# An edge of order on VectorE: each expert block's rest behind the fetched rows already issued

## The chip, the cores and the metric

The kernel runs on one core of a Trainium2 chip. The metric is the device time of one execution in microseconds, the median of several runs. Engines are named as the profile names them: PE (TensorE), DVE (VectorE), ACT (ScalarE), POOL (GpSimd), SP (SyncE).

## The reference

One decoder layer on 1024 tokens of width 1024, in float32, followed by a last RMSNorm. The first half mixes tokens; the second is a retrieval of single-neuron experts, and only that half matters here:

```
def peer(h, w_query, sub_keys1, sub_keys2, expert_down, expert_up):
    q = (hf @ w_query).reshape(T, 8, 2, 128)
    s1, s2 = scores of both halves against 128 keys each
    v1, i1 = top_k(s1, 16); v2, i2 = top_k(s2, 16)
    top_s, pos = top_k(all 256 sums v1 + v2, 16)
    idx = i1 * 128 + i2 at pos          # 16 of 16384 experts, for each of 8 heads
    gates = softmax(top_s)
    # for each token t, over its 8 * 16 = 128 chosen experts e:
    out[t] = sum_e gates[t, e] * gelu(h[t] . expert_down[e]) * expert_up[e]
```

Then x + gate_f * out, and the last norm.

## The kernel before

The 1024 tokens are eight tiles of 128. Two ways of computing the experts run side by side.

Dense tiles (1, 2, 3, 4; 512 tokens). The 16384 experts are 128 blocks of 128. For each block (loop over `units` in `experts`, 1 or 3 blocks to a unit) SP loads the block's down weights (`raw`, L1021) and up weights (`up`, L1029). ACT copies `raw` to float32r (`dnh`, L1023), and DVE takes the rest that this rounding left, `raw - dnh` (`dnl`, L1024): this instruction is what the text calls the rest. PE multiplies (L1033) `dnh` by the high part of h, `dnl` by the high part, `dnh` by the low part, 8 matmuls each, in this order. ACT applies Gelu (L1036), DVE multiplies by the gates (L1037), and one unit later `mm2` (L1007) multiplies by `up`. Half of its outputs stay in PSUM (`res`), the other half (`rot`) are added to SBUF sums by DVE (`ys`, L1014). There are three `raw` buffers and two each of `dnh` and `dnl`.

Fetched tiles (0, 5, 6, 7). For each of a token's 128 experts, one indirect DMA issued by POOL fetches a row of 8 KB (down and up) for each of 128 tokens, so 128 x 8 KB = 1.05 MB: this is what the text calls a row (`gather`, L907). DVE multiplies the down half by h and sums (the dot, L910), ACT applies Gelu and the gate (L911, L912), DVE adds the weighted up half to `yacc` (the add, L903; L901 for the first row of a tile). The add of a row is written in the program after the dot of the next. There are four row buffers (`ROWBUFS` + `MORE`); a row's buffer is free for the next fetch when its add is done. Tile 0 is fetched in `ahead` (half rows), most of it during the first half of the kernel; tiles 5, 6, 7 are fetched beside the dense blocks, 3 x 128 = 384 rows.

What sets the order. Each engine runs its instructions in one fixed order, which the scheduler writes from the priorities of the program. The rows are background work: `drain` takes steps of the generators in `self.bg` at a priority lower by 2000, after each dense block. After b blocks, `min(450 * b / 122, 450)` steps have been issued (L1043 to L1045; `steps` is 129 * 4 - 106 + 40, where 106 is the number of steps of `ahead` that the earlier stages have taken, and NK - SB * LEAD is 122). Those 450 steps are 23 left of `ahead`, 40 of the selections, and 129 for each of the three fetched tiles. Issued means written in the program; the low priority lets the scheduler place a row later than a block written behind it.

After the last block `mm2` runs for the last unit, and `finish` scales, adds and normalises the dense tiles.

Of the kernel before, what the change touches and what calls it, by code (L numbers as in the profile page):

```python
# [6 lines left out]
FT = mybir.dt.float32  # L7
# [6 lines left out]
OP = mybir.AluOpType  # L14
# [3 lines left out]
D = 1024  # L18
# [47 lines left out]
class Trunk:  # L66
    def __init__(self, ctx, tc, I, out):
        self.ctx, self.tc, self.nc, self.I, self.out = ctx, tc, tc.nc, I, out
        self.bg = []
        self.due, self.owed, self.few = 0, 0, 2  # L70
        self.early, self.taken = None, 0

    def pool(self, name, bufs=1, **kw):
        return self.ctx.enter_context(self.tc.tile_pool(name=name, bufs=bufs, **kw))
# [17 lines left out]
    def fetch(self, n):  # L92

        if not self.early or self.pending:
            return
        self.owed += n
        while self.owed >= 1:
            self.owed -= 1
            with self.tc.high_priority(offset=-LATER):
                if next(self.early, None) is None:  # L100
                    return
            self.taken += 1


    def consts(self):
# [782 lines left out]
    def gather(self, j):  # L888

        nc, gp = self.nc, self.gp  # L890
        t = GT[j]
        h2 = gp.tile([128, D], FT, name="h2", bufs=1)
        nc.sync.dma_start(h2, self.h2r[j * 128:(j + 1) * 128, :])
        acc = gp.tile([128, D], FT, name="yacc")
        e = self.eidx[:, j - EARLY].rearrange("p a b -> p (a b)")
        g = self.gates[:, j].rearrange("p a b -> p (a b)")
        prev = None

        def add(u, a, s):
            if s == 0:  # L900
                nc.vector.tensor_scalar(acc, u[:, D:], a, None, op0=OP.mult)  # L901
            else:
                nc.vector.scalar_tensor_tensor(acc, u[:, D:], a, acc, op0=OP.mult, op1=OP.add)  # L903

        for s in range(128):
            u = self.row()
            nc.gpsimd.indirect_dma_start(out=u, out_offset=None, in_=self.I["ud"],  # L907
                                         in_offset=bass.IndirectOffsetOnAxis(ap=e[:, s:s + 1], axis=0))
            a = gp.tile([128, 1], FT, name="act", bufs=4)
            nc.vector.scalar_tensor_tensor(u[:, :D], u[:, :D], 1.0, h2, op0=OP.mult, op1=OP.mult, accum_out=a)  # L910
            nc.scalar.activation(a, a, AF.Gelu)  # L911
            nc.scalar.activation(a, a, AF.Copy, scale=g[:, s:s + 1])  # L912
            if prev is not None:
                add(*prev)
            prev = (u, a, s)
            yield
        add(*prev)
        rows = self.last_rows()
        if j == len(GT) - 1:
            self.kept = rows  # L920
            self.rows.pop()
        xx = self.row()
        self.finish(t, [acc[:, :512], acc[:, 512:]], rows, self.residual(xx[:, :D], t), xx[:, D:])
        yield
# [29 lines left out]
    def experts(self):  # L954

        nc, I = self.nc, self.I
# [10 lines left out]
        def new(kind):  # L967
            return pools[kind].tile(*kinds[kind][:2], name=kind)
# [24 lines left out]
        def mm2(u, ws, some=outs):  # L993
            for o in some:
                t, h = o
                ps = held[o] if o in held else rot.tile([128, 512], FT, name="rot")
                hs = slice(h * 512, (h + 1) * 512)
                ts = slice(t * 128, (t + 1) * 128)
                n = 0
                whole = u == last and o in ysum  # L1000
                if whole:
                    nc.tensor.matmul(ps, self.ident, ysum[o], start=True, stop=False, skip_group_check=True)
                for w, up in ws:
                    st = n == 0 and (u == 0 or o in ysum) and not whole
                    n += 1
                    sp = n == len(ws) and (u == last or o in ysum)
                    nc.tensor.matmul(ps, w[:, ts], up[:, hs], start=st, stop=sp, skip_group_check=True)  # L1007
                if whole:
                    sums[o] = ps
                elif o in ysum:  # L1010
                    if u == 0:
                        nc.vector.tensor_copy(ysum[o], ps)
                    else:
                        nc.vector.tensor_tensor(ysum[o], ps, ysum[o], op=OP.add)  # L1014

        b = 0
        for u, size in enumerate(units):
            ws = []
            for j in range(size):
                raw = new("raw")  # L1020
                nc.sync.dma_start(raw, I["downT"][b])  # L1021
                dn = new("dnh"), new("dnl")
                nc.scalar.activation(dn[0], raw, AF.Copy)  # L1023
                nc.vector.tensor_tensor(dn[1], raw, dn[0].bitcast(FT), op=OP.subtract)  # L1024
                if b % GS == 0:
                    gates = new("gates")
                    nc.sync.dma_start(gates, self.gd[b // GS])
                up = new("up")
                nc.sync.dma_start(up, I["ud"][b * 128:(b + 1) * 128, D:])  # L1029
                p1 = pm1.tile([128, 512], FT, name="m1")  # L1030
                for n, (x, y) in enumerate(((0, 0), (1, 0), (0, 1))):
                    for k in range(KB):
                        nc.tensor.matmul(p1, dn[x][:, k * 128:(k + 1) * 128], h2[y][:, k],  # L1033
                                         start=(k == 0 and n == 0), stop=(k == KB - 1 and n == 2))
                act = new("w")
                nc.scalar.activation(act, p1, AF.Gelu)  # L1036
                nc.vector.tensor_tensor(act.rearrange("p (c t) -> p c t", t=TC),  # L1037
                                        act.rearrange("p (c t) -> p c t", t=TC), gates[:, :, b % GS], op=OP.mult)
                ws.append((act, up))
                if queue and j == (u == last):  # L1040
                    mm2(*queue.pop())
                b += 1
                want = min(steps * b // (NK - SB * LEAD), steps)  # L1043
                self.drain(want - done)
                done = want  # L1045
            queue.append((u, ws))
# [94 lines left out]
```

## Time and profile before

| | |
|---|---|
| time, median of 3 runs | 2900.75 us (2895.56 to 2902.41) |
| the profiled execution's own time | 2912.44 us |
| its span in the trace | 2910.6 us |
| PE busy | 2663.1 us, 91% |
| DVE busy | 2375.6 us, 82% |
| POOL busy | 884.6 us, 30% |
| ACT busy | 830.1 us, 29% |
| moved by DMA | 893.31 MB, mean 307 GB/s |

The profiled execution is one of its own, 11.7 us above the median of the runs; sums are made against its span. The trace gives each instruction's start, duration and line, and the idle time of an engine before it with what ended that idle time. The expert loop begins near 1221 us with the first rest and its last matmuls end near 2891 us.

### The profile page before, as it was taken

Reading aid. Unit: us, or ns where it says so; the run is one execution under the profiler, and the core shown is the slowest. Engines: PE = TensorE matmul, PEld = TensorE weight load, DVE = VectorE, ACT = ScalarE, POOL = GpSimd, SP = SyncE. Lnnn points to the kernel's source line nnn. Section 1 sums busy time; section 2 is a strip of 40 time slices with the busy share of each in tenths; the row PEclk is TensorE's granted clock in tenths of the full one; section 3 lists DMA queues with packets and bytes.
Section 4 is the critical chain, followed back from the end, with each engine's and each line's share of the span. In section 5 each row is a group of like instructions: output and inputs, shape, how many; then the busy total and the mean of one; then the engine's idle time right before and its main releaser. Section 6 shows DMA issues by size and latency. Waiting matters only on the chain. (4 is left out here: it accounts for less than half of the span.)

```text
span 2910.6 us, 31644 instructions
## 1 busy us (share of the span) xinstructions
PE 2663.1 (91%) x10243; PEld 1746.7 (60%) x10244; DVE 2375.6 (82%) x5156; ACT 830.1 (29%) x2244; POOL 884.6 (30%) x679
## 2 busy tenths in 40 slices
PE   8899986789889989699999999999999999999961
PEld 5688555676557876465655666666666666666630
DVE  6625898979999879899999777787877777778887
ACT  3523451322254342322222222222222222222211
POOL 0000066554440005022333333333333333333343
PEclk9999987899989989899999999999999999999985
DMA  8655389999863679888999999899999989998986
GB/s 304 222 172 173 103 296 331 356 362 361 289 234 124 185 220 383 277 310 323 352 354 356 356 366 337 336 364 361 346 348 351 370 320 372 348 368 339 356 320 234
DMA packets 264278, 893.31 MB, mean 307 GB/s; under 512 B 25904, under 2 KB 110000, under 8 KB 212656
## 3 DMA queue, kind: packets, MB, share of 16 engines
q0 software_dynamic: 92448, 541.11, 49.0%
q1 hardware_dynamic: 171664, 350.18, 34.7%
q8 instruction: 81, 1.33, 0.2%
q14 instruction: 85, 0.70, 0.1%
HBM read 840.86 MB, written 50.34 MB: 306 GB/s over the span
## 5 line engine op out<-in xcount | busy, mean ns | idle before, releaser
L907 POOL DMA_INDIRECT row<-in_ud,eidx x384 | 547.5, 1426 | 1105.8 <-DVE yacc L903 870.4
L903 DVE SCALAR_TENSOR_TENSOR yacc<-row,act,yacc 128x1024 f32<-128x1024 f32 x381 | 488.5, 1282 | 67.9 <-ACT act L912 65.1
L910 DVE SCALAR_TENSOR_TENSOR row<-row,h 128x1024 f32<-128x1024 f32 x384 | 467.1, 1218 | 51.1 <-DMA row<-in_ud,eidx 50.8
L1007 PE MATMUL rot<-up,w 128*128 128x512 f32 x1024 | 464.5, 596 | 4.8 <-DVE ys L1014 4.8
L1007 PE MATMUL res<-up,w 128*128 128x512 f32 x1024 | 458.6, 592 | 0.0
L870 POOL DMA_INDIRECT row<-in_ud,eidx x256 | 313.6, 1225 | 417.3 <-DVE rkb L777 102.1
L911 ACT ACTIVATE act<-act 128x1 f32<-128x1 f32 x384 | 77.1, 201 | 976.0 <-DVE row L910 975.6
L1007 PEld LDWEIGHTS rot<-up,w 128*128 128x128 f32 x1024 | 194.9, 191 | 221.8 <-issue 208.3
L1007 PEld LDWEIGHTS res<-up,w 128*128 128x128 f32 x1024 | 193.8, 189 | 200.5 <-issue 189.4
L1033 PE MATMUL m<-h2h,dnh 128*128 128x512 f32 x1024 | 292.9, 427 | 18.9 <-ACT dnh L1023 18.9
L1033 PE MATMUL m<-h2l,dnh 128*128 128x512 f32 x1024 | 285.6, 413 | 0.0
L1033 PE MATMUL m<-h2h,dnl 128*128 128x512 f32 x1024 | 279.6, 412 | 0.0
L1033 PEld LDWEIGHTS m<-h2h,dnh 128*128 128x128 f32 x1024 | 193.5, 189 | 96.8 <-issue 39.5
L307 PE MATMUL acc<-wraw,r 128*128 128x256 f32 x1024 | 239.3, 388 | 8.3 <-ACT s L525 8.3
L435 PE MATMUL acc<-r,wraw 128*128 128x384 f32 (+1 forms) x768 | 235.0, 464 | 2.3 <-ACT s L439 1.3
L581 PE MATMUL acc<-rz,wraw 128*128 128x384 f32 (+1 forms) x768 | 235.3, 457 | 0.0
L1033 PEld LDWEIGHTS m<-h2l,dnh 128*128 128x128 f32 x1024 | 192.6, 188 | 66.5 <-issue 30.4
L1033 PEld LDWEIGHTS m<-h2h,dnl 128*128 128x128 f32 x1024 | 193.4, 189 | 59.2 <-issue 19.1
L307 PEld LDWEIGHTS acc<-wraw,r 128*128 128x128 f32 x1024 | 196.3, 195 | 37.9 <-ACT s L525 9.9
L1014 DVE TENSOR_TENSOR ys<-rot,ys 128x512 f32<-128x512 f32 x168 | 115.4, 687 | 112.1 <-PE rot L1007 111.6
L435 PEld LDWEIGHTS acc<-r,wraw 128*128 128x128 f32 x768 | 147.7, 195 | 81.8 <-issue 8.6
L581 PEld LDWEIGHTS acc<-rz,wraw 128*128 128x128 f32 x768 | 143.7, 194 | 64.0 <-issue 2.3
(298 smaller groups left out, 3271.3 us busy)
## 6 DMA issues: line engine op xcount, KB each, us to landing
up<-in_ud SPq DMA_DIRECT2D x128, 512.0 KB, 7.4
raw<-in_downT SPq DMA_DIRECT2D x128, 512.0 KB, 7.9
gd<-stage SPq DMA_DIRECT2D x32, 1024.0 KB, 9.3
gates<-gd SPq DMA_DIRECT2D x16, 2048.0 KB, 12.3
wraw<-in_w_c SPq DMA_DIRECT2D x48, 512.0 KB, 5.6
wraw<-in_w_q SPq DMA_DIRECT2D x48, 512.0 KB, 6.3
wraw<-in_w_o SPq DMA_DIRECT2D x36, 512.0 KB, 5.2
row<-in_w_ada SPq DMA_DIRECT2D x32, 512.0 KB, 5.3
```

Of the source, the lines that this page charges most:

```text
L307: self.nc.tensor.matmul(acc[i], a(4 * kp + j, slice(i * 128, (i + 1) * 128)), ws[:, j * 256:(j + 1) * 256], start=kp == kps[0] and j == 0 ...
L435: nc.tensor.matmul(acc[:, :T], wc[:, k * 128:(k + 1) * 128], h[:, k], start=k == 0, stop=k == KB - 1)
L581: nc.tensor.matmul(acc[:, :T], wq[:, k * 128:(k + 1) * 128], g[:, k], start=k == 0, stop=k == KB - 1)
L870: nc.gpsimd.indirect_dma_start(out=u[:, i * D:(i + 1) * D], out_offset=None, in_=src, in_offset=bass.IndirectOffsetOnAxis(ap=e[:, s + i:s ...
L903: nc.vector.scalar_tensor_tensor(acc, u[:, D:], a, acc, op0=OP.mult, op1=OP.add)
L907: nc.gpsimd.indirect_dma_start(out=u, out_offset=None, in_=self.I["ud"], in_offset=bass.IndirectOffsetOnAxis(ap=e[:, s:s + 1], axis=0))
L910: nc.vector.scalar_tensor_tensor(u[:, :D], u[:, :D], 1.0, h2, op0=OP.mult, op1=OP.mult, accum_out=a)
L911: nc.scalar.activation(a, a, AF.Gelu)
L1007: nc.tensor.matmul(ps, w[:, ts], up[:, hs], start=st, stop=sp, skip_group_check=True)
L1014: nc.vector.tensor_tensor(ysum[o], ps, ysum[o], op=OP.add)
L1033: nc.tensor.matmul(p1, dn[x][:, k * 128:(k + 1) * 128], h2[y][:, k], start=(k == 0 and n == 0), stop=(k == KB - 1 and n == 2))
```

## The change

An instruction edge of the kind that only sets order (no semaphore, both ends on the same engine) is drawn from each block's rest to the last add of a fetched row that the program has issued before it. `mark` is that last add, L901 or L903; it is None until the first row of tile 5 has been added, so the first blocks get no edge. Rows of tile 0, fetched in `ahead`, don't set it. No instruction is added or taken away.

```diff
+        self.mark = None
...
+    def after(self, ins, prev):
+
+        self.tc.add_manual_dep(ins.ins, prev.ins.name,
+                               mybir.DependencyInfo(mybir.DependencyClass.NoSync, mybir.DependencyReason.DATA),
+                               reason="order")
...
             if s == 0:
-                nc.vector.tensor_scalar(acc, u[:, D:], a, None, op0=OP.mult)
+                self.mark = nc.vector.tensor_scalar(acc, u[:, D:], a, None, op0=OP.mult)
             else:
-                nc.vector.scalar_tensor_tensor(acc, u[:, D:], a, acc, op0=OP.mult, op1=OP.add)
+                self.mark = nc.vector.scalar_tensor_tensor(acc, u[:, D:], a, acc, op0=OP.mult, op1=OP.add)
...
-                nc.vector.tensor_tensor(dn[1], raw, dn[0].bitcast(FT), op=OP.subtract)
+                rest = nc.vector.tensor_tensor(dn[1], raw, dn[0].bitcast(FT), op=OP.subtract)
+
+                if self.mark is not None:
+                    self.after(rest, self.mark)
```

## Rows read from the trace of the kernel before

**Rows 1.** Busy time of all engines by stretch of the expert loop. Columns: stretch and its length in us, busy us and number of instructions of each engine, granted TensorE clock, share of DMA time, GB/s.

```profile
1221.00:1642.00 421.00, 415.87 (x1348) 256.44 (x1349) 392.44 (x934) 102.75 (x255) 126.03 (x92) 0.99 0.91 346
1642.00:1966.80 324.80, 324.80 (x1050) 197.60 (x1048) 251.00 (x323) 76.29 (x206) 111.20 (x77) 1.00 0.91 348
1966.80:2709.40 742.60, 742.60 (x2406) 453.26 (x2405) 578.02 (x729) 175.19 (x471) 245.71 (x174) 1.00 0.92 352
2709.40:2777.40 68.00, 68.00 (x218) 40.85 (x217) 54.92 (x70) 15.59 (x44) 26.15 (x18) 1.00 0.92 350
2777.40:2811.00 33.60, 33.14 (x96) 17.78 (x95) 28.81 (x38) 6.08 (x23) 15.55 (x10) 1.00 0.87 315
2811.00:2881.50 70.50, 0.00 (x0) 0.00 (x0) 54.05 (x68) 10.94 (x44) 29.48 (x19) 0.52 0.88 332
2881.50:2910.60 29.10, 9.43 (x16) 3.87 (x16) 22.58 (x69) 7.07 (x20) 8.95 (x8) 0.62 0.24 92
```

**Rows 2.** Timeline of PE near the end: start us, duration us, line, what it writes and reads, number; in brackets the idle time before it and what ended it.

```profile
2729.47 1.75 PE L1033 MATMUL m<-h2h,dnl 128*128 128x512 f32 x7
2731.06 2.73 PE L1007 MATMUL rot<-up,w 128*128 128x512 f32 x6
...
2735.24 2.74 PE L1007 MATMUL rot<-up,w 128*128 128x512 f32 x6
...
2807.80 2.74 PE L1007 MATMUL rot<-up,w 128*128 128x512 f32 x6
2881.54 2.07 PE L1002 MATMUL rot<-ys,ident 128*128 128x512 f32 x2 [71.00 <-DVE dnl L932]
```

**Rows 3.** The adds (L903) by stretch: stretch, length, busy us and number on DVE, clock, DMA share, GB/s.

```profile
0.00:1642.00 1642.00, 111.15 (x87) 0.94 0.79 279
1642.00:1966.80 324.80, 93.51 (x73) 1.00 0.91 348
1966.80:2709.40 742.60, 218.89 (x171) 1.00 0.92 352
2709.40:2777.40 68.00, 21.91 (x18) 1.00 0.92 350
```

**Rows 4.** The first adds of a tile (L901) by stretch, the same columns.

```profile
0.00:1966.80 1966.80, 1.49 (x2) 0.95 0.81 291
1966.80:2709.40 742.60, 0.75 (x1) 1.00 0.92 352
```

**Rows 5.** The rests (L1024) by stretch, the same columns; a rest cut by a bound counts on both sides.

```profile
0.00:1642.00 1642.00, 43.79 (x36) 0.94 0.79 279
1642.00:1966.80 324.80, 31.75 (x26) 1.00 0.91 348
1966.80:2709.40 742.60, 74.45 (x60) 1.00 0.92 352
```

**Rows 6.** Timeline of DVE: the rest of block 62, the rest of block 122, and one add and two pairs of adds after PE's last dense matmul.

```profile
1966.86 1.22 DVE L1024 TENSOR_TENSOR dnl<-raw,dnh 128x1024 fp32r<-128x1024 f32 x1 [0.25 <-ACT dnh L1023]
...
2709.45 1.22 DVE L1024 TENSOR_TENSOR dnl<-raw,dnh 128x1024 fp32r<-128x1024 f32 x1
...
2812.53 2.68 DVE L903 SCALAR_TENSOR_TENSOR yacc<-row,act,yacc 128x1024 f32<-128x1024 f32 x2
...
2842.34 1.28 DVE L903 SCALAR_TENSOR_TENSOR yacc<-row,act,yacc 128x1024 f32<-128x1024 f32 x1 [0.60 <-ACT act L912]
...
2877.06 2.68 DVE L903 SCALAR_TENSOR_TENSOR yacc<-row,act,yacc 128x1024 f32<-128x1024 f32 x2
```

**Rows 7.** Timeline of POOL: the fetch that the add at 2842.34 us releases.

```profile
2843.90 1.68 POOL L907 DMA_INDIRECT row<-in_ud,eidx  x1 [1.24 <-DVE yacc L903]
```

**Rows 8.** Waits in the stretch 1967 to 2709 us: who waited for whom, us in total, times, longest.

```profile
POOL row L907 <- DVE yacc L903: 468.9, 157, 11.7
...
DVE ys L1014 <- PE rot L1007: 73.0, 46, 5.0
DVE yacc L903 <- ACT act L912: 37.6, 63, 0.6
DVE w L1037 <- ACT w L1036: 30.8, 23, 2.8
DVE row L910 <- DMA row<-in_ud,eidx: 11.3, 11, 2.2
...
DVE dnl L1024 <- ACT dnh L1023: 6.7, 27, 0.3
```

**Rows 9.** Groups of DVE instructions in the stretch 1966.8 to 2709.4 us: busy us, mean ns of one, idle time before them and what ended it.

```profile
L903 DVE SCALAR_TENSOR_TENSOR yacc<-row,act,yacc 128x1024 f32<-128x1024 f32 x171 | 219.0, 1281 | 38.7 <-ACT act L912 37.6 <-DVE yacc L903 0.5
L910 DVE SCALAR_TENSOR_TENSOR row<-row,h 128x1024 f32<-128x1024 f32 x172 | 209.4, 1219 | 11.5 <-DMA row<-in_ud,eidx 11.3
L1024 DVE TENSOR_TENSOR dnl<-raw,dnh 128x1024 fp32r<-128x1024 f32 x60 | 74.5, 1241 | 7.5 <-ACT dnh L1023 6.7
L1014 DVE TENSOR_TENSOR ys<-rot,ys 128x512 f32<-128x512 f32 x80 | 55.1, 689 | 73.4 <-PE rot L1007 73.0
L1037 DVE TENSOR_TENSOR w<-w,gates 128x512 f32<-128x512 f32 x60 | 41.4, 689 | 31.5 <-ACT w L1036 30.8
```

**Rows 10.** DMA in the stretch 1966.8 to 2709.4 us: bytes and rate, the rate in 40 slices of 18.6 us, and issues with their size and median us from issue to landing.

```profile
GB/s 407 289 423 329 365 296 387 324 425 301 363 296 414 350 343 301 401 339 408 329 345 314 329 304 426 370 351 305 428 349 336 313 396 297 427 313 369 295 381 336
DMA packets 44019, 261.31 MB, mean 352 GB/s; under 512 B 4891, under 2 KB 4891, under 8 KB 21057
...
raw<-in_downT SPq DMA_DIRECT2D x60, 512.0 KB, 9.0
...
row<-in_ud,eidx POOLq DMA_INDIRECT x171, 8.6
```

**Rows 11.** DMA in the stretch 2811 to 2881 us, the same view.

```profile
DMA packets 3413, 23.35 MB, mean 334 GB/s; under 512 B 378, under 2 KB 378, under 8 KB 747
...
row<-in_ud,eidx POOLq DMA_INDIRECT x19, 7.9
```

## The prediction

> **What bounds the kernel now.** I read the busy times by stretch first. From block 62 on PE is busy all the time: 742.6 of 742.6 us between the rests of blocks 62 and 122, 12.4 us a block, at a granted clock of 1.00 [rows 1, 5, 6]. DVE is busy 578 us of that, 78%. Then PE does nothing for 70.5 us, from 2811 to 2881.5 us, while DVE works on rows, and 29.1 us of last matmuls and normalisation follow [rows 1, 2]. So two things bound the kernel in turn: PE in the loop, the fetched rows behind it. What can be won is the gap of 71 us.
>
> In the loop DVE is not held by its own work. Its idle time goes to PE (ys 73.0 us, and w 30.8 us behind Gelu, which waits for PE), 37.6 us to the row's Gelu, and only 11.3 us to rows that have not landed [rows 8]. POOL waits 468.9 us for adds to free a buffer [rows 8]. So rows are paced by four buffers and by a DVE that stands in line behind PE.
>
> **What the edge holds back.** It costs no instruction and no semaphore. Its effect is the place of the rest among the adds, and that can be counted. When the rest of block 62 starts, DVE has done 87 + 73 + 2 = 162 adds [rows 3, 4, 5]. The program has by then issued 450 * 62 / 122 = 228 steps; less 23, 40 and 129 that leaves 36 of the second tile, and with the add one row behind, 128 + 35 = 163 adds. So up to there the scheduler already has the rows about where the edge wants them, ahead of it earlier on, and the edge should change nothing. At block 122 the program has issued all 384 adds; DVE has done 162 + 172 = 334 [rows 3, 4]. So the edge pulls 50 rows in front of the rest of block 122: between the two rests 222 rows must pass where 172 do now. That excludes the rival that the edge does nothing.
>
> What waits behind a held rest: on DVE, the block's gate and the sums behind it; on PE, 16 of the block's 24 first matmuls and everything after them. The rest of block 122 now ends 18.8 us before PE needs it [rows 2, 6], so some 20 us of slack are used up before PE stops. On SP the load of `raw` three blocks later waits for the rest, and the loads of `up`, gates and h queue behind it; three buffers cover a landing of 9.0 us [rows 10] at 12 us or more a block, so I cost it at nothing, and at up to 9 us a block if that cover went.
>
> **What is won and lost.** Let R be the time of a row between the two rests. The rest of block 122 comes at 1967 + 222 R. Behind it no row is left, and PE finds the rest just done. Now it takes 201.2 us from that rest to the end (2910.6 - 2709.4). Then: 1.5 us for the rest, the 81.0 us of PE work from 2729.5 to 2810.5 [rows 2], less 5.5 us of `rot` matmuls of the earlier unit, which PE will have done while it waited [rows 2], plus the 29.1 us of the end [rows 1]: 106 us. So the end gains 95 us (of which the 71 us gap is the larger part and the lead of the rest the other), and the loop loses 222 R - 742.6. The change is 222 R - 837.5 us, zero at R = 3.77. PE alone allows 742.6 / 222 = 3.35; today's R is 742.6 / 172 = 4.32.
>
> **What R will be.** Take one buffer's round, four rows long. Today 4 * 4.32 = 17.3 us: 0.3 from the end of the add to the issue [rows 6, 7], 8.6 to the landing [rows 10], so 8.4 at DVE. With PE still, after 2811 us, five rounds take 2877.06 - 2812.53 = 64.5 us [rows 6], 12.9 a round or 3.23 a row: 0.3, 7.9 [rows 11] and 4.7 at DVE. The 3.7 us between the two DVE parts are waits for PE (73.0 + 30.8 + 6.7 = 110.5 us with the wait for dnh) and DVE's other work (74.5 + 55.1 + 41.4 = 171 us) [rows 8, 9]; shared out in that ratio, 1.4 and 2.2. When the rows are late, PE waits for DVE and not DVE for PE, so the 1.4 goes; the other work is spread over 222 rows for 172, 1.7. The round is then 0.3 + 8.6 + 4.7 + 1.7 = 15.3 us, R = 3.83. But more rows in the same time also load the DMA: the stretch must carry 261.3 MB [rows 10] plus 50 * 1.05, 314 MB, 1.41 MB a row, 369 GB/s at that R against 352 now. From the two landings (7.9 us at 334 GB/s, 8.6 at 352, [rows 10, 11]) a GB/s costs 0.04 us, an estimate; with it the round settles at 3.92. I take the middle, R = 3.87, since the landing in the tail differs in more than its rate. Then 222 * 3.87 = 859 us, and the change is +21.6 us: the span goes to 2932 us, and the median, 11.7 us lower than the profiled time, to 2922 us.
>
> The bounds of R. Below: the other work fits wholly into the waits for rows, 13.6 us a round, 3.40, and 3.70 with the dearer landing. Above: the waits for PE stay as well, since DVE's order is fixed and a gate that stands too early makes all rows behind it wait: 17.3 - 0.5 = 16.8, R = 4.19.
>
> The DMA as a bound of its own: slices of 18.6 us reach 405 to 428 GB/s, others between them 290 to 310 [rows 10]. At 428 the 314 MB take 733 us, less than PE needs; at the mean of today, 891 us, R = 4.01. So the transfers neither exclude a gain nor make it safe. The Trainium skill (Perfetto Trace Analysis, Roofline) gives 358 GB/s as a core's share of HBM and about 435 GB/s as what its 16 DMA engines carry when it is alone; the slices agree with the second as a peak, and no stretch here holds it for long. By 435 the sum would be PE's pace and 2830 us; by 358, 877 us, 2940 us.
>
> **The rivals.** *Rows keep close to PE's pace* (faster). The place is the landing-to-dot wait: if DVE's other work falls into the gaps in which it would wait for a row, R is 3.40 to 3.70. At 3.70 the change is -16 us; below 3.45 PE is the bound again and the whole gap of 71 us is won, 2830 us. Middle: R = 3.61, -36 us, 2865 us. It decides from R = 3.77 down. For it: the 405 to 428 GB/s slices, and only 11.3 us of waits for rows now. Against: four buffers and a landing of 8.6 us leave little. The Trainium skill (Perfetto Trace Analysis, Optimization Strategy) holds that interleaving regimes with different busiest engines can pay; that is this rival, and the idle PE of the tail agrees that there are two regimes. Chance 0.31.
>
> *A draw*: R between 3.73 and 3.81; within 9 us of 2901. Chance 0.16.
>
> *The forecast*: R from 3.81 to 4.07, 2909 to 2966 us. Chance 0.40.
>
> *DVE stays in line behind PE*: R = 4.19, 222 * 4.19 - 837.5 = +93 us, 2994 us. Against it: a PE that waits for the rest has done everything else. For it: gates stand a fixed number of rows behind their rest, and PE needs two groups of 8 matmuls, Gelu and ACT's turn before the gate can run. Chance 0.13.
>
> **How the numbers follow.** Faster by over 0.3% is the first rival, 0.31; within 0.3% (about what a measurement of this kernel can tell from no change) the draw, 0.16; slower the last two, 0.53. The range takes R from 3.57 (-45 us) to 4.17 (+88 us): 2856 to 2988 us. It leaves out the whole gap won and the worst of the last case, about 0.1 on either side.
>
> **What would show it.** Up to block 60, about 1940 us, both traces alike. From there DVE's waits for ys and w shrink, its waits for rows grow, and PE shows gaps of 1 to 2 us a block with the rest (dnl) as releaser; all 384 adds stand before the rest of block 122; no gap of 71 us; the last six blocks run at PE's pace with DVE half idle. The number to read is the time between the rests of blocks 62 and 122: 859 us forecast, 838 is even. I am wrong if PE shows no waits for dnl (R held at 3.35), if that time is over 900 us with DVE waiting for ACT w (DVE still behind PE), or if the time behind the rest of block 122 isn't near 106 us.

## The result and the profile after

The changed kernel takes 2943.41 us (median of 4 runs, 2933.23 to 2944.37) against 2899.61 us for the kernel before, timed beside it (median of 4 runs). The ratio of the means is 1.0144, 95% interval 1.0119 to 1.017: it is slower. Its profiled execution spans 2941.2 us, 30.6 us more than the span shown of before; the medians lie 43.8 us apart, since the profiled execution of before was 12.8 us above its median (2912.44 to 2899.61 us) and that of after is 0.4 us below.

Line numbers are up by 7 to 10: the add is L910 (L908 for a tile's first), the dot L917, the fetch L914, `mm2` L1014, `ys` L1021, `dnh` L1030, the rest L1031, the first matmuls L1043, Gelu L1046, the gate L1047.

Busy time of all engines by stretch of the expert loop, columns as in [rows 1]. The first rest is at 1214.6 us; the last line runs from the rest of block 122 to the end, the one above it from the rest of block 62 to that of block 122.

```profile
1214.60:1634.10 419.50, 414.89 (x1349) 255.78 (x1350) 391.83 (x934) 102.91 (x256) 127.50 (x92) 0.99 0.91 347
1634.10:1960.30 326.20, 326.20 (x1057) 198.86 (x1056) 252.19 (x324) 76.55 (x206) 109.39 (x77) 1.00 0.91 348
...
1960.33:2848.52 888.19, 801.20 (x2479) 472.69 (x2478) 698.42 (x882) 199.42 (x568) 335.94 (x221) 0.98 0.91 353
2848.50:2941.20 92.70, 79.06 (x248) 46.41 (x246) 38.19 (x90) 13.93 (x30) 7.85 (x8) 0.94 0.22 78
```

The adds (L910) in the same bounds; the last line is an add cut by the bound:

```profile
0.00:1960.33 1960.33, 206.51 (x161) 0.95 0.82 292
1960.33:2848.52 888.19, 282.20 (x221) 0.98 0.91 353
2848.52:2941.20 92.68, 0.08 (x1) 0.94 0.22 78
```

Up to block 62 the two kernels are alike: 161 + 2 = 163 adds stand before that rest (162 in [rows 3, 4]), and PE has no idle time in the stretch before it. From there the edge acts. The 60 blocks take 888.2 us where they took 742.6, PE is idle for 87 us of them, and DVE is busy 120 us longer. Behind the rest of block 122 there are 92.7 us where there were 201.2, and no row is left.

DVE at the two rests (its timeline, as [rows 6]), then PE behind the second (as [rows 2]):

```profile
1959.12 1.28 DVE L910 SCALAR_TENSOR_TENSOR yacc<-row,act,yacc 128x1024 f32<-128x1024 f32 x1 [0.67 <-ACT act L919]
1960.33 1.22 DVE L1031 TENSOR_TENSOR dnl<-raw,dnh 128x1024 fp32r<-128x1024 f32 x1
...
2845.92 2.68 DVE L910 SCALAR_TENSOR_TENSOR yacc<-row,act,yacc 128x1024 f32<-128x1024 f32 x2
2848.52 2.35 DVE L1031 TENSOR_TENSOR dnl<-raw,dnh 128x1024 fp32r<-128x1024 f32 x2
```

```profile
2844.69 3.70 PE L1014 MATMUL res<-up,w 128*128 128x512 f32 x8 [1.41 <-DVE w L1047]
...
2851.79 1.99 PE L1043 MATMUL m<-h2h,dnl 128*128 128x512 f32 x8
...
2910.23 1.02 PE L1009 MATMUL rot<-ys,ident 128*128 128x512 f32 x2
2911.09 2.74 PE L1014 MATMUL rot<-up,w 128*128 128x512 f32 x6
```

The matmul that stood behind 71.00 us of idle PE in [rows 2] (`rot<-ys,ident`) now follows its neighbours without a gap, among the last expert matmuls. The edge did what it says: the rows' tail is gone.

Waits between the two rests, as [rows 8]:

```profile
POOL row L914 <- DVE yacc L910: 503.5, 183, 10.5
...
DVE yacc L910 <- ACT act L919: 64.8, 107, 0.7
DVE w L1047 <- ACT w L1046: 64.5, 36, 4.9
PE res L1014 <- DVE w L1047: 41.0, 26, 3.8
DVE row L917 <- DMA row<-in_ud,eidx: 32.6, 24, 5.5
PE m L1043 <- ACT dnh L1030: 24.6, 14, 2.8
DVE ys L1021 <- PE rot L1014: 24.4, 23, 4.6
PE m L1043 <- DVE dnl L1031: 21.4, 7, 9.6
```

DVE's waits for `ys` fell by 48.6 us and those for `dnh` by 6.7, but the waits for Gelu in front of the gate grew by 33.7, those for a row's Gelu by 27.2 and those for rows not landed by 21.3. DVE was idle 164.5 us in this stretch before; it is idle 189.8 us now, with more work to do. PE waits 87 us: 41.0 for the gate, 24.6 for `dnh` and 21.4 for the rest. All 14 waits for `dnh` look alike: when PE has done a block's first matmuls, ACT runs that block's Gelu (0.60 us) and only then the copy to `dnh` (1.05 us) that PE needs next.

### The profile page after: what moved, and what is told of

Read it like the earlier page. It is cut to its first block, busy times and chain, and to the rows that moved or that the text cites. A ratio compares the mean times of both kernels' runs of the same rounds, so it can differ in the third digit from the quotient of the medians.

```text
span 2941.2 us, 31662 instructions
## 1 busy us (share of the span) xinstructions
PE 2679.1 (91%) x10243; PEld 1742.5 (59%) x10244; DVE 2375.5 (81%) x5156; ACT 828.9 (28%) x2244; POOL 910.7 (31%) x679
## 4 chain that ended last, share of the span: by engine, by line
PE 52%; DVE 22%; DMA 9%; issue 9%; POOL 4%; ACT 3%; SPq 0%; POOLq 0%; DVEq 0%; ACTq 0%
PE m L1043 15%; PE res L1014 9%; PE rot L1014 9%; PE acc L314 7%; DMA row<-in_ud,eidx 7%; PE acc L588 5%; DVE yacc L910 3%; POOL row L914 3%; DVE row L882 2%; DVE row L917 2%; PE acc L442 2%; PE g L850 1%; DVE s L477 1%; DVE yacc L886 1%; POOL row L877 1%
## 5 line engine op out<-in xcount | busy, mean ns | idle before, releaser
L914 POOL DMA_INDIRECT row<-in_ud,eidx x384 | 567.6, 1478 | 1060.4 <-DVE yacc L910 817.9
L910 DVE SCALAR_TENSOR_TENSOR yacc<-row,act,yacc 128x1024 f32<-128x1024 f32 x381 | 488.8, 1283 | 84.1 <-ACT act L919 80.3
L917 DVE SCALAR_TENSOR_TENSOR row<-row,h 128x1024 f32<-128x1024 f32 x384 | 467.4, 1220 | 60.4 <-DMA row<-in_ud,eidx 60.1
L1014 PE MATMUL res<-up,w 128*128 128x512 f32 x1024 | 470.7, 604 | 41.0 <-DVE w L1047 41.0
L1014 PE MATMUL rot<-up,w 128*128 128x512 f32 x1024 | 466.3, 593 | 4.5 <-DVE ys L1021 4.5
L877 POOL DMA_INDIRECT row<-in_ud,eidx x256 | 322.2, 1259 | 400.6 <-DVE rkb L784 102.1
L1014 PEld LDWEIGHTS res<-up,w 128*128 128x128 f32 x1024 | 195.1, 193 | 260.1 <-issue 195.3
L1043 PE MATMUL m<-h2h,dnh 128*128 128x512 f32 x1024 | 297.8, 432 | 43.8 <-ACT dnh L1030 43.8
L1014 PEld LDWEIGHTS rot<-up,w 128*128 128x128 f32 x1024 | 193.7, 190 | 222.1 <-issue 206.9
L1043 PE MATMUL m<-h2h,dnl 128*128 128x512 f32 x1024 | 286.0, 420 | 21.4 <-DVE dnl L1031 21.4
L1043 PE MATMUL m<-h2l,dnh 128*128 128x512 f32 x1024 | 272.9, 405 | 0.0
L1043 PEld LDWEIGHTS m<-h2h,dnh 128*128 128x128 f32 x1024 | 193.9, 191 | 128.2 <-ACT dnh L1030 50.6
L1043 PEld LDWEIGHTS m<-h2h,dnl 128*128 128x128 f32 x1024 | 195.1, 191 | 90.7 <-DVE dnl L1031 27.8
L1043 PEld LDWEIGHTS m<-h2l,dnh 128*128 128x128 f32 x1024 | 194.4, 190 | 54.7 <-issue 15.3
L1021 DVE TENSOR_TENSOR ys<-rot,ys 128x512 f32<-128x512 f32 x168 | 115.0, 688 | 76.4 <-PE rot L1014 75.9
```

Source lines behind the costliest of these rows:

```text
L877: nc.gpsimd.indirect_dma_start(out=u[:, i * D:(i + 1) * D], out_offset=None, in_=src, in_offset=bass.IndirectOffsetOnAxis(ap=e[:, s + i:s ...
L910: self.mark = nc.vector.scalar_tensor_tensor(acc, u[:, D:], a, acc, op0=OP.mult, op1=OP.add)
```

## The experiments

Unless said otherwise an edit is made to the changed kernel. Each run's stretch from the rest of block 62 to that of block 122 is shown as one line, with the columns of [rows 1]; "the loop" below is this stretch. The kernel before was timed again beside each group of runs. Where no interval is given there is a single run.

The theory of the prediction was the round of four buffers: a row's time is landing, DVE's part and what stands between. Its rivals in the expectations are DVE's fixed order (it waits for Gelu and PE wherever it is put) and a DMA that is full. From the lagged edges on a simpler one is tried: the loop has no free room, and each pulled row is paid for at once.

### How much of the edge: a series of lags

The edge is drawn not to the last add issued but to one some rows older. With `marks` a list of all adds:

```diff
-                if self.mark is not None:
-                    self.after(rest, self.mark)
+                if len(self.marks) > 24:
+                    self.after(rest, self.marks[-1 - 24])
```

*Lag 24.*

> The edge drawn not to the last add issued but to the one 24 adds earlier. In the kernel before, the scheduler is 24 adds short of the issued ones near block 92, so the edge should act from there on only: 30 blocks at 14.8 us instead of 12.4 cost 73 us. At block 122 it asks for 360 adds instead of 334; the 24 rows left run beside the last six blocks (75 us of PE, 24 * 3.23 = 78 us of rows), so most of the gap of 71 us and of the 20 us of lead are won. Theory A and B alike (the loss goes with the number of blocks held, the gain with the tail): 2875 to 2900 us, against 2943 with the edge as it is and 2900 without. If any held rest were costly in itself, it would be as slow as the full edge.

```profile
1957.85:2777.33 819.48, 783.23 (x2491) 470.35 (x2490) 642.78 (x811) 189.03 (x522) 288.11 (x200) 0.99 0.92 353
2777.33:2890.10 112.77, 80.46 (x244) 46.08 (x242) 96.06 (x162) 26.00 (x78) 42.79 (x30) 0.88 0.77 285
...
2862.21 2.08 PE L1009 MATMUL rot<-ys,ident 128*128 128x512 f32 x2 [13.13 <-DVE dnl L939]
```

2894.39 us (8 runs) against 2904.85 (11 runs), ratio 0.9968, 0.9949 to 0.9987: a little faster than the kernel before. Its PE still has one gap of 13.1 us at the end.

*Lag 12* (a single run).

> The edge to the add 12 rows earlier. It should act from block 76 on (46 blocks at 14.8 us for 12.4: 110 us lost) and leave 12 rows for the last six blocks, which then run at PE's pace: about 104 us won. 2895 to 2920 us, between the 2894 us of 24 rows earlier and the 2943 us of the full edge; if the loss does not go with the number of blocks held, near one of the two.

```profile
1959.28:2811.11 851.83, 788.41 (x2491) 472.05 (x2490) 669.20 (x847) 194.19 (x546) 321.38 (x212) 0.98 0.92 355
2811.11:2903.70 92.59, 78.64 (x244) 45.58 (x242) 66.08 (x126) 19.68 (x54) 23.17 (x18) 0.95 0.55 209
```

2905.45 us against 2899.78. The line to see is the second: 12 rows are left behind the rest of block 122, and the end takes 92.6 us, as long as with none. They are free there.

*Lag 32.*

> The edge 32 adds behind the last issued one instead of 24 or 0. It acts from about block 98. Eighteen rows are pulled forward by block 122 at 2.9 us, some 55 us, and the end behind block 122 shortens from 201 us to about 130 us: 2880 to 2895 us if pulled rows cost the same everywhere, and within 10 us of 2900 us if the series (2943 at lag 0, 2905 at 12, 2894 at 24, 2900 with no edge) already has its best near 24.

```profile
1951.09:2747.18 796.09, 777.02 (x2490) 469.33 (x2489) 623.28 (x787) 185.05 (x506) 272.95 (x192) 1.00 0.92 353
2747.18:2886.40 139.22, 80.74 (x244) 46.21 (x242) 115.69 (x186) 29.97 (x94) 53.76 (x38) 0.81 0.78 291
```

2895.39 us (10 runs) against 2902.15 (19 runs), ratio 0.9981, 0.997 to 0.9992.

*A lag that grows from block 60 on*, 0.6 rows a block, so that the pull is spread evenly:

```diff
-                if self.mark is not None:
-                    self.after(rest, self.mark)
+                late = max(0, int(0.6 * (b - 60)))
+                if len(self.marks) > late:
+                    self.after(rest, self.marks[-1 - late])
```

> The edge asks from block 60 on for 0.6 adds a block less than are issued, 3.09 a block instead of 3.69: 347 adds at the rest of block 122, against 334 without an edge and 384 with the full one. With the full edge a block takes 14.8 us and carries 3.69 rows, without it 12.4 us and 2.87. If DVE's line has room that only its order leaves unused (PE-bound with spare time on DVE), 13 rows more cost nothing and shorten the tail by 13 * 3.23 us: 2855 to 2870 us. If the loop pays for each row pulled forward, in proportion between those two points (2.9 us a row), the loss is about 38 us and the gain 42 us and a part of the lead: 2885 to 2905 us.

```profile
1953.93:2740.87 786.94, 770.91 (x2475) 467.11 (x2474) 608.55 (x770) 183.29 (x496) 287.14 (x188) 1.00 0.91 350
2740.87:2896.20 155.33, 87.12 (x260) 49.62 (x258) 127.53 (x202) 32.44 (x104) 59.53 (x42) 0.78 0.79 297
```

2899.35 us (10 runs) against 2899.78 (13 runs), ratio 1.0002, 0.9985 to 1.0019. An even, gentle pull isn't free either: with 13 rows more between the two rests the loop is 44 us longer, and PE, which had no idle time there before, is idle for 16 us of it.

### Rows or blocks: the full edge from block 100 on

```diff
-                if self.mark is not None:
+                if self.mark is not None and b >= 100:
```

> The full edge, but only for blocks 100 to 127; every block up to 99 is as in the kernel before. Law A, the loop pays for each row that is pulled forward (2.9 us a row: 146 us for 50 rows in the full edge's run): the rows that the edge has to pull by block 122 are the same 50, so the loss is nearly the same, only gathered in front of block 100: 62 to 122 again 860 to 900 us, total 2920 to 2950 us, with one long wait of PE for the rest of block 100 (30 rows or so late, 60 to 100 us). Law B, the loop pays for each block whose rest is held (146 us over 60 blocks, 2.4 us each): 22 held blocks before 122 cost 54 us, 62 to 122 is near 795 us and the total near 2850 us, a gain.

A single run: 2940.61 us against 2902.15. Its loop, the part of it from the rest of block 92 to that of block 104, the end, and PE's timeline at the rest of block 100:

```profile
1958.02:2846.02 888.00, 783.79 (x2486) 470.95 (x2485) 700.01 (x882) 201.16 (x570) 325.57 (x221) 0.95 0.92 354
...
2328.78:2586.95 258.17, 177.89 (x559) 106.02 (x557) 203.96 (x263) 54.67 (x168) 104.79 (x71) 0.85 0.91 346
...
2846.02:2938.80 92.78, 79.27 (x249) 46.54 (x247) 38.14 (x90) 13.94 (x30) 7.82 (x8) 0.94 0.22 78
```

```profile
2538.05 3.78 PE L1043 MATMUL m<-h2h,dnl 128*128 128x512 f32 x8 [75.32 <-DVE dnl L1031]
```

Now PE stops once, for 75.3 us, and nowhere else for the rest by more than 2 us; with the full edge it stops in many small gaps. The loop is as long to 0.2 us (888.0 and 888.2). So the price hangs on the number of rows that are pulled in front of block 122, not on the number of blocks that are held nor on how the stops are spread.

### The series together

From the lines above and [rows 1, 5]; rows are adds that start between the two rests, DVE idle is length less busy, and the last columns are taken against the kernel before.

| kernel | rows in the loop | loop us | DVE busy | DVE idle | loop's price of a pulled row | behind rest 122 | loop lost, end gained |
|---|---|---|---|---|---|---|---|
| before | 172 | 742.6 | 578.1 | 164.5 | | 201.2 | |
| growing lag | 185 | 786.9 | 608.6 | 178.4 | 44.3/13 = 3.4 | 155.3 | 44.3, 45.9 |
| lag 32 | 190 | 796.1 | 623.3 | 172.8 | 53.5/18 = 3.0 | 139.2 | 53.5, 62.0 |
| lag 24 | 198 | 819.5 | 642.8 | 176.7 | 76.9/26 = 3.0 | 112.8 | 76.9, 88.4 |
| lag 12 | 210 | 851.8 | 669.2 | 182.6 | 109.2/38 = 2.9 | 92.6 | 109.2, 108.6 |
| full edge | 221 | 888.2 | 698.4 | 189.8 | 145.6/49 = 3.0 | 92.7 | 145.6, 108.5 |
| from block 100 | 222 | 888.0 | 700.0 | 188.0 | 145.4/50 = 2.9 | 92.8 | 145.4, 108.4 |

Two things are to be seen. A pulled row makes the loop 2.9 to 3.4 us longer: in the full edge some 2.45 us of DVE's own instructions (120.3 us more for 49 rows) and some 0.5 us of idle time; the 164 to 190 us in which DVE is idle are never used up. And the end gets shorter by 3.4 us a row for the first 26 (88.4/26), by 1.7 for the next 12 (20.2/12), by nothing for the last 11 or 12. Lost less gained is -1.6, -8.5, -11.5, +0.6, +37.1 and +37.0 us; the timed runs lie -0.4, -6.8, -10.5 (medians), +5.7, +43.8 and +38.5 us from the kernel before.

Part of both prices is neither loss nor gain. With an edge the rests come nearer to the matmuls that need them, and PE does 69 to 85 matmuls more between the two rests than the 2406 of before (2475 to 2491). At 742.6/2406 = 0.31 us each, 21 to 26 us of PE's work have moved from the end into the loop; in lost less gained this drops out. Without it a pulled row costs the loop 1.8, 1.5, 1.9, 2.2, 2.5 and 2.4 us, in the order of the table: no row is free, but the first ones are cheaper, and the 23 rows between lag 24 and the full edge cost some 3.1 us each. The end then gains 2.4 us a row for the first 26.

One rival fits this series as well. In all seven kernels the loop moves 350 to 355 GB/s, and a row's 1.05 MB at 353 GB/s take 2.97 us, just what a pulled row adds to the loop. A DMA at its limit would look like that; the runs with five buffers and with half the bytes, below, bear on it.

### What holds the loop: single runs with parts of it changed

*The gate left out.* Its multiplication is removed, so the dense tiles are summed without gates.

```diff
-                nc.vector.tensor_tensor(act.rearrange("p (c t) -> p c t", t=TC),
-                                        act.rearrange("p (c t) -> p c t", t=TC), gates[:, :, b % GS], op=OP.mult)
```

> The changed kernel without the multiplication by the gates in the dense blocks (so the dense tiles' result is another one). DVE loses 60 instructions of 0.7 us in the stretch between the rests of blocks 62 and 122 (43 us) and the 64.5 us that it waited there for Gelu before them. Theory A (the round of four buffers): the waits turn up as waits for rows, the stretch loses little more than the share of the 43 us that stood in a row's way, 840 to 870 us of 888. Theory B (DVE's line): the stretch falls by both, to 770 to 790 us. Theory C (the DMA is full at 353 GB/s): 880 to 890 us, nothing changes.

Its loop, and two of DVE's waits in it:

```profile
1993.83:2822.17 828.34, 765.71 (x2406) 450.00 (x2405) 653.52 (x815) 195.97 (x564) 331.18 (x221) 0.99 0.93 359
...
DVE yacc L910 <- ACT act L919: 85.1, 94, 3.0
DVE row L917 <- DMA row<-in_ud,eidx: 78.9, 55, 5.8
```

What DMA moved in the loop, in the changed kernel and then without the gate:

```profile
DMA packets 51557, 313.78 MB, mean 353 GB/s; under 512 B 5725, under 2 KB 5725, under 8 KB 22491
DMA packets 50094, 297.44 MB, mean 359 GB/s; under 512 B 5564, under 2 KB 5564, under 8 KB 21923
```

2915.62 us, with the rest of block 62 33.5 us later than in the changed kernel. 44.9 us of work left DVE and the loop fell by 59.9, to a length between the bands of theories A and B. Two things besides the gate went with it. The loads of `gates`, seven of 2048 KB, are gone too; with three loads of `up` that fall outside, the loop moves 16.3 MB less, which at 353 GB/s is 46 us. So this run says nothing against a full DMA. And the loop holds 2406 matmuls for 2479, so some 22.5 us of the fall are PE's work that lies outside it. The 64.5 us of waits in front of the gate are gone with it, but DVE's idle time falls only from 189.8 to 174.8: its waits for rows go from 32.6 to 78.9 us, for a row's Gelu from 64.8 to 85.1.

*A fifth row buffer, and two `raw` buffers for three* (the room has to come from somewhere).

```diff
-MORE = 1
+MORE = 2
...
-                  "raw": ([128, D], FT, 3), "dnh": ([128, D], FR, 2), "dnl": ([128, D], FR, 2),
+                  "raw": ([128, D], FT, 2), "dnh": ([128, D], FR, 2), "dnl": ([128, D], FR, 2),
```

> The changed kernel with five row buffers instead of four; to make room there are two buffers for raw instead of three. The round of a buffer was 4 * 4.02 = 16.1 us. Theory A: the same round shared by five, R = 3.2 to 3.4, so PE's pace again, 745 to 790 us between the rests of blocks 62 and 122 (888), a span near 2850 us. Theory B (DVE's line): at most the 32.6 us of waiting for rows go, 855 to 890 us. Theory C (the DMA is full): 870 to 890 us. If the raw buffer that was given up matters, PE waits for ACT dnh, which now takes 24.6 us in that stretch.

```profile
2006.64:2850.66 844.02, 768.76 (x2408) 458.08 (x2407) 690.03 (x877) 201.04 (x567) 343.12 (x220) 0.98 0.95 370
```

2948.61 us. The loop is 44.2 us shorter, and DVE's idle time falls by 36 (154.0 us left). Half of the 44.2 is the 71 matmuls that this loop holds fewer (2408 for 2479), 21.9 us, and the rest of block 62 comes 46.3 us later than with four buffers, so nothing is left of it. PE's pace, which theory A expected, did not come back. The buffers are one part of the price, and in the loop alone. The loop runs at 370 GB/s here, so 353 is no fixed ceiling of the DMA.

*Both together*, edits as above.

> The changed kernel with both: no multiplication by the gates (the dense tiles' result is another one) and five row buffers with two of raw. Alone, the first took the stretch between the rests of blocks 62 and 122 from 888 to 828 us and raised DVE's waits for rows from 33 to 79 us; the second took it to 844 us with 11 us of waits for rows and 65 us for the gate's Gelu. If the two limits stand close behind each other (DVE's line and the round of four), together they reach PE's pace: 742 to 775 us. If they only share one slack, 815 to 830 us.

```profile
2034.58:2834.17 799.59, 766.31 (x2411) 460.73 (x2409) 653.84 (x818) 199.27 (x567) 354.65 (x220) 0.98 0.96 372
```

2932.23 us, the rest of block 62 74 us later than in the changed kernel. The loop fell by 88.6 us, between the two expected bands: the single steps (59.9 and 44.2, each with some 22 us of PE's moved work) add to 104.1, with that work counted once to some 82, so neither hides the other. DVE is still idle 145.7 us.

*Half the bytes of a row*: only 4 KB for each token are fetched, and dot and add both work on that half.

```diff
-            nc.gpsimd.indirect_dma_start(out=u, out_offset=None, in_=self.I["ud"],
+            nc.gpsimd.indirect_dma_start(out=u[:, :D], out_offset=None, in_=self.I["ud"].rearrange("e (a d) -> (e a) d", d=D),
```

> The changed kernel with rows of 4 KB instead of 8 KB: the fetch brings half the bytes, and both DVE instructions of a row work on that half (so the up halves of the experts are not read, and the output is another one). DVE's work is the same instruction for instruction. Read is the time between the rests of blocks 62 and 122, 888 us in the changed kernel, of which DVE is busy 698 and waits 32.6 for rows. Theory A (the round of four buffers, with the landing in it, sets the pace): the landing gets cheaper by a quarter or more, the round with it, and PE's pace comes back: 745 to 800 us. Theory B (DVE's own line sets it: 698 us of work, 64.8 waiting for the row's Gelu, 64.5 for the gate's Gelu, 24.4 for rot): only the 32.6 us of waiting for rows go, 840 to 860 us. Theory C (the DMA is full at 353 GB/s, the rate of that stretch before and after the change): 198 MB are left of 314, PE's pace, 742 to 760 us, at a DMA share well under 0.9.

```profile
2043.23:2874.56 831.33, 762.96 (x2370) 457.32 (x2369) 600.33 (x777) 181.12 (x494) 258.88 (x186) 0.97 0.62 214
```

2998.94 us. The DMA engines carry 214 GB/s at a share of 0.62, and a row takes longer (184 rows, 4.52 us each). In this kernel a full DMA isn't what sets the time, and the loop's 831.3 us lie in none of the three bands. More can't be read from it: the scheduler wrote another order (200 rows were done at the rest of block 62, where the changed kernel has 163).

### Moving DVE's waits

*A late gate*: the gate of a block is written behind the rows of one more block, with an edge to the last of them; its old place behind Gelu goes.

```diff
+                gate = nc.vector.tensor_tensor(act.rearrange("p (c t) -> p c t", t=TC),
+                                               act.rearrange("p (c t) -> p c t", t=TC), gates[:, :, (b - 1) % GS], op=OP.mult)
+                if self.mark is not None:
+                    self.after(gate, self.mark)
```

> The full edge, and the gate multiplication of a block stands behind the fetched rows of one more block (its own edge of the same kind), so that DVE comes to it later. If DVE's waits for Gelu in front of the gate (64.5 us between the rests of blocks 62 and 122) are what a fixed order costs DVE, they go and the stretch falls from 888 us to 825 to 845 us, total 2880 to 2900 us. If DVE only stands in line for PE at another place, or PE then waits for the gate, the stretch stays at 870 to 890 us and the time at 2925 to 2945 us, with the wait of PE's second multiplication for the gate (41 us) grown by as much as the other shrank.

```profile
1962.79:2839.53 876.74, 798.05 (x2472) 469.96 (x2471) 694.21 (x882) 198.76 (x568) 312.38 (x221) 0.97 0.91 357
```

```profile
DVE yacc L910 <- ACT act L919: 104.9, 105, 6.2
PE res L1014 <- DVE w L1054: 53.8, 22, 6.2
DVE row L917 <- DMA row<-in_ud,eidx: 51.1, 38, 6.7
```

2937.24 us, a single run. DVE's waits in front of the gate (64.5 us) are gone from the list, and those for a row's Gelu grew by 40, those for rows by 18.5 us. DVE is idle 182.5 us for 189.8: the wait was moved, not removed. My theory that the gate's place holds DVE up falls.

*Lag 24 and a late gate.*

> The edge 24 adds behind, as in the earlier run at 2894 us, and the gate behind the rows of one more block with the same lag. If a late gate frees DVE, the waits for Gelu (44 us in the stretch of the earlier run) go and the total is 2860 to 2885 us, faster than both kernels. If the wait only moves, 2890 to 2910 us.

```profile
1963.14:2789.97 826.83, 785.42 (x2475) 468.92 (x2474) 642.09 (x810) 188.72 (x524) 279.27 (x201) 0.98 0.91 350
```

2899.32 us (10 runs) against 2902.15 (19 runs), ratio 0.999, 0.998 to 0.9999: no better than lag 24 alone, whose interval (0.9949 to 0.9987) it overlaps. Here too the wait only moved.

### The rest on POOL

Made to the kernel before, with no edge, to see what the loop does when DVE has less to do.

```diff
-                nc.vector.tensor_tensor(dn[1], raw, dn[0].bitcast(FT), op=OP.subtract)
+                nc.gpsimd.tensor_tensor(dn[1], raw, dn[0].bitcast(FT), op=OP.subtract)
```

> The kernel before (no edge) with the rest computed by POOL instead of DVE. Theory B (DVE's line paces the rows): DVE is rid of 128 instructions of 1.14 us, 146 us in all, of which 68 lie in the stretch of blocks 62 to 122; the rows move up, the tail of 71 us shrinks to under 30 us: 2850 to 2875 us. Against it: POOL takes 1.6 us for 512 columns of such a sum, so over 3 us for a rest, and stands in line with the fetches, which wait for buffers; a rest behind a fetch that waits is the edge again, by another engine: 2900 to 2950 us, with PE waiting for dnl from POOL. Theory A (the round of four buffers): 0.4 ms of POOL's time come into the round's issue, the rows slow down: over 2910 us.

Busy times (as [rows 1]) and groups of DVE, then of POOL, between the same two rests; last PE's gap behind the last block:

```profile
1990.54:2730.07 739.53, 739.53 (x2396) 451.85 (x2396) 622.09 (x664) 173.24 (x464) 406.68 (x234) 1.00 0.93 350
...
L903 DVE SCALAR_TENSOR_TENSOR yacc<-row,act,yacc 128x1024 f32<-128x1024 f32 x170 | 300.7, 1769 | 52.9 <-ACT act L912 51.7
L910 DVE SCALAR_TENSOR_TENSOR row<-row,h 128x1024 f32<-128x1024 f32 x170 | 240.2, 1415 | 15.2 <-DMA row<-in_ud,eidx 15.1
...
L1024 POOL TENSOR_TENSOR dnl<-raw,dnh 128x1024 fp32r<-128x1024 f32 x61 | 156.0, 2558 | 39.1 <-ACT act L911 29.1 <-ACT dnh L1023 8.9 <-issue 0.2
...
2901.83 2.08 PE L1002 MATMUL rot<-ys,ident 128*128 128x512 f32 x2 [70.85 <-DVE dnl L932]
```

2935.54 us (4 runs), ratio 1.013, 1.0103 to 1.0158. DVE was to lose 74.5 us in the loop [rows 9] and gained 44 (622.1 us busy for 578.1): an add takes 1769 ns beside POOL's rest and 1281 without [rows 9], a dot 1415 for 1219. It doesn't test the loop, since DVE has more to do and not less; PE's gap behind the last block stays (70.9 us). Nor does the loop get longer: it takes 739.5 us with PE busy all the time. The time is lost ahead of it, where the rest of block 62 starts at 1990.5 us for 1966.9. So the total lies in the band of 2900 to 2950 us, but without the PE waits for `dnl` in this stretch that the band was argued from.

## Why the prediction was right, and where its sizes were off

*Where the edge acts, and how many rows it pulls*: shown, 163 adds at the rest of block 62 and none left behind that of block 122.

*The tail goes*: shown. The end was put at 106 us and is 92.7. The term that was off is the 5.5 us of matmuls that PE would have done ahead: 2479 matmuls lie between the two rests for 2406 before, 73 more, some 22.5 us at 0.31 us each. The other terms of the end came out some 4 us longer.

*The loop's price*: put at 859 us (R = 3.87), measured 888.2 (4.02). The step that was mis-sized is "When the rows are late, PE waits for DVE and not DVE for PE, so the 1.4 goes": those waits fell only from 110.5 to 88.9 us (`ys` 24.4, Gelu 64.5), and waits for rows and for rows' Gelu grew by 48.5. So here PE and DVE wait for each other in turn, and with the late gate DVE's waits changed their place and stayed. PE's 24.6 us of waits for `dnh` have no term in the prediction; the load of `raw`, put at nothing, was right, for nothing in the loop waits for it. The rival that kept these waits whole (R = 4.19) went too far the other way. R of 3.87 was reached late: from the rest of block 104 (317 adds done) to that of 122, 259.5 us for 67 rows, while the 154 rows before took 628.7 us, 4.08 each. Why the two halves differ was not tried.

*The sum for the profiled execution*: loop +145.6 (forecast +116.4, 859 less 742.6), end -108.5 (forecast -95), and the part up to block 62 6.5 us shorter with nothing changed in it (in the lagged kernels it varies from 1951.1 to 1963.1 us): +30.6, for a forecast of +21.6. That these differ by only 9 us is in part luck: the loop was 29 us longer than forecast, the end 13 and the first part 6.5 us shorter. Taking 11.7 us off for the median cost the forecast the rest of the 21 us by which it is low: what sets the profiled execution of before apart did not repeat in that of after.

*The rivals.* PE's pace (R 3.40 to 3.70) fell: DVE's other work did not fall into its waits. Two regimes there were, but interleaving them paid only for the rows that PE was really idle for. The DMA as a bound: the Trainium skill (Perfetto Trace Analysis, Roofline) puts a core's share of HBM at 358 GB/s when both cores of a pair draw on it. By that rate the forecast would have been 2940 us, close to the result. As a ceiling the runs don't bear it out: with five buffers the loop ran at 370 GB/s over 844 us, with five buffers and no gate at 372 over 800, and with rows of half the bytes a row took 4.52 us for 4.02. But with four buffers and whole rows no loop went above 359 GB/s, and no run tells whether the transfers or the round of the buffers hold it there: this rival is weakened, not excluded.

*The signs.* PE's waits were to have the rest as releaser. It is so for 21.4 of 87 us; the largest part (41.0) waits for the gate, which stands behind the rest on DVE and so is late with it. DVE's waits for `w` were to shrink and grew from 30.8 to 64.5 us. Of the signs of being wrong, the loop stayed under its 900 us by 12 us, and the end missed its 106 us by 13.

What decides is in the series. By it the loop had little room for more rows even before the change: the first 13 to 18 cost it 1.5 to 1.8 us each, PE's moved work left out, and the last 23 some 3.1. Of the 50 rows left behind the rest of block 122, about 12 beside the last six blocks were free, and the end paid for those in PE's idle time. Pulling 26 of the second kind wins some 0.4 us a row (11.5 us by the traces, 10.5 by the medians); pulling the first kind costs its full price and gains nothing, and the full edge does both. That the full edge's price is made of DVE's 2.45 us and 0.5 us of idle time a row is measured. Why DVE's 165 to 190 us of idle time can't be filled is shown only so far that with five buffers there are 36 fewer and with a late gate 7. The rest stays open, the DMA's part in it too.

## What to carry to other kernels

Idle time of an engine is not free room. Here DVE was idle for 22% of the loop, and more rows still did not fit in for nothing: price the next unit by measuring what it adds, not by the idle share. When two stretches are compared between the same marks, see that the same work lies between them: here the marks themselves moved against PE's work. Pull work forward only as far as it would stand in an idle tail; what runs beside the last blocks was free where it was. An edge with an adjustable lag measures both prices in a few runs, and its best is where they meet (lags 24 and 32 here, 2894 and 2895 us, which the intervals don't separate).

## What was not expected of the hardware

DVE and POOL hold each other up. In the run with the rest on POOL a subtraction of two 128x1024 operands takes 2558 ns in the mean, and DVE's adds go from 1281 to 1769 ns. The mean hides two kinds: of the adds between the two rests the 118 that overlap no POOL subtraction take 1.28 us, and the 51 that do take 2.90. Two pairs from the timeline, the first with DVE held, the second with POOL held:

```profile
2316.75 3.71 DVE L903 SCALAR_TENSOR_TENSOR yacc<-row,act,yacc 128x1024 f32<-128x1024 f32 x1
2316.98 2.39 POOL L1024 TENSOR_TENSOR dnl<-raw,dnh 128x1024 fp32r<-128x1024 f32 x1
...
2500.89 1.22 DVE L910 SCALAR_TENSOR_TENSOR row<-row,h 128x1024 f32<-128x1024 f32 x1
2501.19 3.17 POOL L1024 TENSOR_TENSOR dnl<-raw,dnh 128x1024 fp32r<-128x1024 f32 x1 [1.36 <-ACT act L911]
```

The held add ends 1.09 us behind POOL's end, which is nearly its whole length: one waits for the other, they don't share. The Trainium skill (SBUF — State Buffer, Who interferes with whom) says that a DVE instruction with two SBUF inputs contends with a GpSimd instruction that reads SBUF; the runs agree, and the mean price was 170 rows by 0.49 us on the adds and 0.20 us on the dots, 116 us, against the 74.5 us taken off DVE.

PE's clock after the 75.3 us stop of the run from block 100: the eight matmuls that took 1.99 us in the changed kernel's timeline took 3.78, the lower of the two levels (1.2 for 2.4 GHz). The granted clock of these 3.8 us was 0.50, that of blocks 92 to 104 0.85. In the full edge, with 87 us of stops in small gaps, the loop's clock stayed at 0.98.
